# Two query tiles' attention weights turned in one PSUM bank, and the second group's sample scores asked for between the two turns

## The chip, the core and the metric

The kernel runs on one core of one Trainium2 chip. The core has five engines that run side by side, each through its own list of instructions in order: TensorE (PE in the profile; its weight loads are shown apart as PEld), VectorE (DVE), ScalarE (ACT), GpSimd (POOL) and SyncE (SP, which issues DMAs). They wait for one another through semaphores. The metric is the device time of one execution in microseconds (us).

## The reference, cut to what matters

One step of a two-layer encoder: a recurrent layer, then a layer of stick-breaking attention with 16 heads of 128, over 512 prompt rows and over 8 sample sequences of 16 rows, each with 512 cached rows. The change lies in the attention:

```python
def sb_block(q, q_pos, k, v):
    z = jnp.einsum('bqhd,bshd->bhqs', q, k).astype(jnp.float32) * (HEAD_DIM ** -0.5)
    mask = jnp.arange(k.shape[1])[None, :] < q_pos[:, None]
    log_keep = jnp.where(mask, jax.nn.log_sigmoid(-z), 0.0)
    log_after = lax.cumsum(log_keep, axis=3, reverse=True) - log_keep
    attn = jnp.where(mask, jnp.exp(jax.nn.log_sigmoid(z) + log_after), 0.0)
    o = jnp.einsum('bhqs,bshd->bqhd', attn, v.astype(jnp.float32))
    return o.astype(q.dtype)
# prompt: q, k, v of its own 512 rows; sample b: k, v of cache_k[b], cache_v[b] and 16 new rows
# y = (o * silu(zg)) @ w_out, where q and zg come from hn @ w_in
```

## The kernel before

The attention goes head by head. While one head's attention runs, TensorE also computes the next head's query and gate columns (`query`, a generator; its products are the matmuls `psh`, each 128x320, in fp32r with high and low parts, three matmuls for one product). `heads` walks a list of letters, `ORDER` for heads 0 to 14 and `LAST` for head 15, and calls one step for each letter:

- `q`: the next piece of the generator.
- `P` (`prompt_scores`): scores z3, z2, z1 of the four query tiles of 128 rows and, in z1, of the sample rows against their new keys; `sticks` then makes weights e of them (absolute value, exp, log on ScalarE, a scan and two subtractions on VectorE, exp on ScalarE, a mask on POOL). e3 holds query tile 3, e2 tile 2 and, in its last 128 columns, tile 0, and e1 tile 1.
- `S0`, `S1` (`sample_scores`): scores of 4 sample sequences against their cached keys (`zc`, tiles `ck`), and their weights by `sticks`.
- `V0`, `V1` (`prompt_turn`): the weights are turned (transposed through TensorE against `ident`) by `spread`: into a PSUM bank `pa`, split from there into a high part `ath` (ScalarE) and a low part `atl` (VectorE). V0 turns query tiles 3 and 2, V1 tiles 0 and 1.
- `O` (`prompt_out`): the prompt's output `po`, 12 matmuls over key blocks 0 to 3; block 0 reads row 0 of `ath` and `atl`, block 1 row 1, and so on.
- `T0`, `T1` (`sample_turn`): issues the loads of a group's cached values (`cv`, two tiles of 512 KB, two buffers, on SP's queue), turns the group's weights into banks `pas` (copied to `at` by ScalarE) and `pan` (copied to `an` by VectorE).
- `M0`, `M1` (`sample_out`): the group's output `pos`, first from `vn` and `an`, then 16 matmuls from `cv` and `at`. `C0`, `C1` (`sample_close`): turned back through `pot`, times the gate.
- `L`, `U`, `N`, `K`, `W`: loads and splits of the next head's keys and values (`kr`, `vr`, `ck`).

`pa`, `pas`, `pan`, `po`, `pos` and `pot` all come from one ring of two PSUM banks (`bank`, tag "one"). A bank is free again when its last reader is done. The letters are not the engines' order: a scheduler with costs and priorities of its own merges all steps into one list for each engine and picks, for each bank asked for, the one that it expects free. That is why the order is shown below from the built programs.

Of the kernel before, what the change touches and what calls it, by code (L numbers as in the profile page):

```python
# [11 lines left out]
F32 = mybir.dt.float32  # L12
F32R = mybir.dt.float32r
BF16 = mybir.dt.bfloat16
AF = mybir.ActivationFunctionType
ALU = mybir.AluOpType
# [3 lines left out]
P = 128  # L20
# [25 lines left out]
X12, X22, X11, S1, S2, S3, S4 = range(7)  # L46
# [4 lines left out]
class Trunk:  # L51
# [705 lines left out]
    S0 = 3 + TP  # L757
# [924 lines left out]
    def attention(self, h, ap, qkv, zs):  # L1682

        nc, I, O = self.nc, self.I, self.O
        V, A, mm, tr = nc.vector, nc.scalar, nc.tensor.matmul, nc.tensor.transpose
        kw = dict(skip_group_check=True)
        dma = nc.sync.dma_start
        one = self.bank
        zt = lambda n: self.ring("quad", 4, n)
        pd = "p (t d) -> p t d"  # L1690
# [9 lines left out]
        ath = ap.tile([P, 3, 512], F32R, tag="ath", name="ath", bufs=1)  # L1700
        atl = ap.tile([P, 3, 512], F32R, tag="atl", name="atl", bufs=1)

        def spread(e, i):

            ps = one("pa")
            for j in range(i + 1):
                tr(ps[:, P * j : P * j + P], e[:, P * j : P * j + P], self.ident)
            n = min(i + 1, 3)
            src = ps[:, : P * n].rearrange(pd, d=P)
            for sv, hv, lv in [(src, ath[:, :n, P * i : P * i + P], atl[:, :n, P * i : P * i + P])] + (  # L1710
                [(ps[:, 384:], ath[:, 1, 0:P], atl[:, 1, 0:P])] if i == 3 else []
            ):
                A.activation(hv, sv, AF.Copy)
                V.tensor_tensor(lv, sv, hv.bitcast(F32), ALU.subtract)


        def sample_scores(g):
# [10 lines left out]
        def new_values(g):  # L1728
            t = ap.tile([TS, 4, P], F32, tag="vn", name="vn", bufs=1)
            dma = (nc.gpsimd if g else nc.sync).dma_start  # L1730
            rows = O["v"][TP + 64 * g : TP + 64 * g + 64, P * h : P * h + P]
            dma(t, rows.rearrange("(b t) d -> t b d", t=TS))
            return t
# [72 lines left out]

        def prompt_turn(late):
            if late:
                spread(st["e2"][:, 384:], 0)
                spread(st["e1"], 1)  # L1810
            else:
                spread(st["e3"], 3)
                spread(st["e2"], 2)
# [12 lines left out]
        st = {"vn": new_values(0)}  # L1826
        steps = {"P": prompt_scores, "O": prompt_out}
        for g in range(2):
            steps[f"V{g}"] = lambda g=g: prompt_turn(g)
            steps[f"T{g}"] = lambda g=g: sample_turn(g)  # L1830
            steps[f"M{g}"] = lambda g=g: sample_out(g)
            steps[f"C{g}"] = lambda g=g: sample_close(g)
            steps[f"S{g}"] = lambda g=g: sample_scores(g)
# [2 lines left out]

    STAY = (NHEAD - 2,)
    LAST = "P S0 q q q S1 V0 q V1 q Z T0 M0 O q C0 q T1 q M1 q C1 q"
    ORDER = "P q q S0 L q q V0 V1 S1 T0 O U q M0 q T1 N K q C0 M1 W q C1"

    def heads(self, count=NHEAD):
        with self.pool("att") as ap:
# [10 lines left out]
            for h in range(count):  # L1853
# [3 lines left out]
                qn = self.query(h + 1, ap) if more else out  # L1857
                for step in (self.ORDER if more else self.LAST).split():
                    if step == "q":
# [152 lines left out]
```

## Time and profile before

| what | value |
|---|---|
| runs | 2860.42 us median of 3 (2860.24 to 2861.73) |
| profiled execution | 2859.51 us, its span 2857.4 us |
| PE busy | 2791.4 us, 98% of the span |
| VectorE, ScalarE, POOL busy | 71%, 58%, 15% |
| granted TensorE clock over the span | 0.995 |
| PE busy, 2230 to 2270 us (inside the heads) | 39.86 of 40.00 us |

The heads lie between about 2030 and 2640 us; one takes 39 us. PE works through them nearly without a gap, so the wait rows of PE and of its weight loads tell what is still open there. Line numbers (L1707) are those of the kernel before; L108 to L110 are the three matmuls of a product, L1707 the transposes of `spread`, L1713 and L1714 its splits, L1721 `zc`, L1745 and L1749 `pas` and `pan`, L1757 and L1762 `pos`, L1737 the loads of `cv`. In the changed kernel the lines behind `spread` are some nine higher.

### The profile page before, as it was taken

To read this page: it belongs to the slowest core of one execution; us is meant where nothing else is said; L and a number is where in the kernel's file an instruction comes from. 1 tells how busy PE (TensorE), PEld (TensorE's weight loads), DVE (VectorE), ACT (ScalarE), POOL (GpSimd) and SP (SyncE) were. 2 spreads that over 40 slices of the span, in tenths; PEclk is the share of its full clock that TensorE was granted. 3 is DMA by queue.
4 is the path that set the end of the run, shared out by engine and by line. 5 is a ranking of instruction groups with operands and counts; after the bars stand their busy time and mean duration, and the time that the engine had idled before them with its cause. 6 is when DMAs were issued, how large, how long until landed. Compare 5 with 4: busy or idle time off the path is not lost.

```text
span 2857.4 us, 48071 instructions
## 1 busy us (share of the span) xinstructions
PE 2791.4 (98%) x18340; PEld 2463.5 (86%) x18340; DVE 2033.8 (71%) x3344; ACT 1667.7 (58%) x2846; POOL 415.1 (15%) x684
## 2 busy tenths in 40 slices
PE   6899999999999999999999999999999999999998
PEld 5799999999999987777787899966889888887887
DVE  7677777777677766766866766667877877776335
ACT  5467556656566655665656555553666766666223
POOL 0021212122122211112220000001111111011000
PEclk9999999999999999999999999999999999999999
DMA  8966776667666666676786333574566666668637
GB/s 326 330 145 153 165 167 154 148 167 162 160 152 158 152 226 203 202 251 192 228 277 207 104 109 105 181 276 168 165 197 195 195 197 185 208 193 287 194 111 228
DMA packets 249094, 544.49 MB, mean 191 GB/s; under 512 B 23496, under 2 KB 108616, under 8 KB 247712
## 3 DMA queue, kind: packets, MB, share of 16 engines
q1 hardware_dynamic: 208528, 402.22, 43.6%
q0 software_dynamic: 40336, 139.21, 20.5%
q8 instruction: 144, 2.36, 0.3%
q14 instruction: 86, 0.70, 0.1%
HBM read 499.97 MB, written 41.37 MB: 189 GB/s over the span
## 4 chain that ended last, share of the span: by engine, by line
PE 80%; DVE 4%; ACT 4%; DMA 2%; issue 2%; POOL 0%; DVEq 0%; POOLq 0%; SPq 0%; ACTq 0%
PE acc L108 7%; PE acc L110 7%; PE acc L109 7%; PE pa L108 4%; PE pa L110 4%; PE pa L109 4%; PE psh L108 3%; PE psh L110 3%; PE psh L109 3%; PE pc L110 3%; PE pc L108 3%; PE pc L109 3%; PE acck L108 2%; PE acck L109 2%; PE acck L110 2%
## 5 line engine op out<-in xcount | busy, mean ns | idle before, releaser
L108 PE MATMUL acc<-wh,yh 128*128 128x512 f32 x940 | 370.3, 395 | 1.7 <-DVE e L1642 1.6
L109 PE MATMUL acc<-wl,yh 128*128 128x512 f32 x940 | 367.4, 391 | 0.4 <-DVE wl L94 0.4
L110 PE MATMUL acc<-wh,yl 128*128 128x512 f32 x940 | 366.2, 390 | 1.3 <-DVE yl L958 1.3
L94 DVE TENSOR_TENSOR wl<-wr,wh 128x1024 fp32r<-128x1024 f32 x151 | 186.6, 1238 | 217.6 <-ACT wh L93 216.9
L93 ACT ACTIVATE wh<-wr 128x1024 fp32r<-128x1024 f32 x151 | 159.5, 1057 | 264.7 <-PE acc L110 214.3
L108 PEld LDWEIGHTS acc<-wh,yh 128*128 128x128 f32 x940 | 176.6, 188 | 55.5 <-issue 16.1
L110 PEld LDWEIGHTS acc<-wh,yl 128*128 128x128 f32 x940 | 176.8, 188 | 38.6 <-DVE yl L958 1.7
L109 PEld LDWEIGHTS acc<-wl,yh 128*128 128x128 f32 x940 | 177.0, 188 | 37.5 <-DVE wl L94 1.1
L193 DVE TENSOR_TENSOR wa<-wa 128x1024 f32<-128x1024 f32 (+1 forms) x160 | 191.4, 1247 | 9.3 <-ACT wa L192 8.9
L110 PE MATMUL pa<-xs,wl 128*128 128x320 f32 x630 | 194.8, 309 | 0.5 <-DVE wl L94 0.5
L109 PE MATMUL pa<-xs,wh 128*128 128x320 f32 x630 | 194.7, 309 | 0.0
L108 PE MATMUL pa<-xs,wh 128*128 128x320 f32 x630 | 194.7, 309 | 0.0
L93 ACT ACTIVATE wh<-sum 128x896 fp32r<-128x896 f32 x102 | 96.8, 949 | 142.3 <-PE pa L109 46.5
L192 ACT ACTIVATE wa<-wa 128x1024 bf16<-128x1024 f32 x160 | 159.2, 1046 | 22.5 <-DVE wa L193 12.4
L542 POOL DMA_DIRECT2D sum<-w_in_a_dram x90 | 79.1, 882 | 498.2 <-DVE wl L94 237.7
L108 PE MATMUL psh<-nh,wl 128*128 128x320 f32 x480 | 150.8, 314 | 0.5 <-DVE z L1529 0.5
L110 PE MATMUL psh<-nh,wl 128*128 128x320 f32 x480 | 150.1, 313 | 0.0
L109 PE MATMUL psh<-nl,wl 128*128 128x320 f32 x480 | 149.4, 311 | 0.0
L93 ACT ACTIVATE wh<-rv 128x256 fp32r<-128x256 f32 (+1 forms) x108 | 51.8, 479 | 144.9 <-PE pa L109 92.3
L108 PE MATMUL acck<-wh,nh 128*128 128x512 f32 x320 | 127.5, 399 | 3.9 <-ACT nh L1163 2.2
L110 PE MATMUL pc<-xs,wl 128*128 128x320 f32 x420 | 129.8, 309 | 0.7 <-DVE wl L94 0.7
L108 PE MATMUL pc<-xs,wh 128*128 128x320 f32 x420 | 130.1, 310 | 0.0
(489 smaller groups left out, 8583.5 us busy)
## 6 DMA issues: line engine op xcount, KB each, us to landing
wa<-w_ada_dram SPq DMA_DIRECT2D x120, 512.0 KB, 6.1
wr<-w_out_a_dram SPq DMA_DIRECT2D x96, 512.0 KB, 4.5
sum<-w_in_a_dram POOLq DMA_DIRECT2D x90, 448.0 KB, 5.8
wa<-w_ada_dram POOLq DMA_DIRECT2D x72, 512.0 KB, 4.9
wr<-w_in_b_dram SPq DMA_DIRECT2D x64, 512.0 KB, 4.3
ck<-cache_k_dram SPq DMA_DIRECT2D x64, 512.0 KB, 5.0
cv<-cache_v_dram SPq DMA_DIRECT2D x64, 512.0 KB, 5.7
wr<-w_out_b_dram SPq DMA_DIRECT2D x55, 512.0 KB, 3.9
```

What stands on the lines that cost most here:

```text
L93: self.split_at = nc.scalar.activation(hi[:, :n], raw, AF.Copy).ins
L94: nc.vector.tensor_tensor(lo[:, :n], raw, hi[:, :n].bitcast(F32), ALU.subtract)
L108: mm(out, sh, mh, start=start, stop=False, **kw)
L109: mm(out, sh, ml, start=False, stop=False, **kw)
L110: return mm(out, sl, mh, start=False, stop=stop, **kw)
L192: nc.scalar.activation(parts[i], raw, AF.Copy)
L193: nc.vector.tensor_tensor(parts[2] if i else raw, raw, parts[i], ALU.subtract)
L542: self.nc.gpsimd.dma_start(self.big[tag], self.quarter(w, i), accum_op=ALU.add)
```

## The change

V1's two turns (tile 0 from e2, tile 1 from e1) put their three transposes into one bank instead of two. The splits from there are cut otherwise: first 256 columns, which are row 0 of `ath` and `atl` for tiles 0 and 1, then the 128 columns of row 1. And in `ORDER` the letter S1 goes ahead of V1 (`LAST` has that order already).

```diff
+        def parts(pairs):
+            for sv, hv, lv in pairs:
+                A.activation(hv, sv, AF.Copy)
+                V.tensor_tensor(lv, sv, hv.bitcast(F32), ALU.subtract)
+
         def spread(e, i):
             ps = one("pa")
             for j in range(i + 1):
                 tr(ps[:, P * j : P * j + P], e[:, P * j : P * j + P], self.ident)
-            n = min(i + 1, 3)
-            src = ps[:, : P * n].rearrange(pd, d=P)
-            for sv, hv, lv in [(src, ath[:, :n, P * i : P * i + P], atl[:, :n, P * i : P * i + P])] + (
-                [(ps[:, 384:], ath[:, 1, 0:P], atl[:, 1, 0:P])] if i == 3 else []
-            ):
-                A.activation(hv, sv, AF.Copy)
-                V.tensor_tensor(lv, sv, hv.bitcast(F32), ALU.subtract)
+            src = ps[:, :384].rearrange(pd, d=P)
+            parts([(src, *(x[:, :3, P * i : P * i + P] for x in (ath, atl)))]
+                  + [(ps[:, 384:], ath[:, 1, 0:P], atl[:, 1, 0:P])] * (i == 3))
+
+        def spread_first(e0, e1):
+            ps = one("pa")
+            for n, e in enumerate((e0, e1[:, :P], e1[:, P:])):
+                tr(ps[:, P * n : P * n + P], e, self.ident)
+            parts([(ps[:, : 2 * P], ath[:, 0, : 2 * P], atl[:, 0, : 2 * P]),
+                   (ps[:, 2 * P : 3 * P], ath[:, 1, P : 2 * P], atl[:, 1, P : 2 * P])])
...
             if late:
-                spread(st["e2"][:, 384:], 0)
-                spread(st["e1"], 1)
+                spread_first(st["e2"][:, 384:], st["e1"])
...
-    ORDER = "P q q S0 L q q V0 V1 S1 T0 O U q M0 q T1 N K q C0 M1 W q C1"
+    ORDER = "P q q S0 L q q V0 S1 V1 T0 O U q M0 q T1 N K q C0 M1 W q C1"
```

On TensorE, from V0's turns to the second group's `pas`, as in each of the heads 1 to 13; the query matmuls `psh` are left out where the dots stand. Before, there are 5, 5, 5, 4, 1, none and 16 of them in the seven gaps (the one behind the first `po` row holds only the other rows of `po`, and `pos` from `vn`):

```order
L1707 MATMUL pa<-ident,e 128x128 x7
L1721 MATMUL zc<-ck,qs 32x512 x4
...
L1707 MATMUL pa<-ident,e 128x128
...
L1707 MATMUL pa<-ident,e 128x128 x2
...
L1745 MATMUL pas<-ident,e 128x128 x4
...
L1749 MATMUL pan<-ident,e 16x128
...
L108 MATMUL po<-ath,vh 128x512
...
L1762 MATMUL pos<-cv,at 32x128 x16
...
L1745 MATMUL pas<-ident,e 128x128 x4
```

The same stretch of the changed kernel, with 5, 4, 5, 5, none, 10, none and 7 `psh` in the gaps:

```order
L1712 MATMUL pa<-ident,e 128x128 x7
L1730 MATMUL zc<-ck,qs 32x512 x4
...
L1721 MATMUL pa<-ident,e 128x128 x3
...
L1754 MATMUL pas<-ident,e 128x128 x4
...
L1758 MATMUL pan<-ident,e 16x128
...
L108 MATMUL po<-ath,vh 128x512
...
L108 MATMUL po<-ath,vh 128x384
...
L109 MATMUL po<-atl,vh 128x384
...
L1771 MATMUL pos<-cv,at 32x128 x16
...
L1754 MATMUL pas<-ident,e 128x128 x4
```

`zc` stays where it was, V1's transposes stand together, ten `psh` stand inside `po`, and of the 36 `psh` from `zc` to the second `pas` 29 are ahead of the first `pos` instead of 20.

On VectorE, from the 256-wide low split of V1 on, head 4 (`e<-zc` and `e<-z` are the second group's sample weights, `e<-keep` their scan, `wh` and `wr` the next head's query weights):

```order
L1714 TENSOR_TENSOR atl<-pa,ath 128x2x128
L1363 TENSOR_TENSOR wh<-wr,wh 128x512
L1636 SCALAR_TENSOR_TENSOR e<-z_22268,e 128x16
L1751 COPY an<-pan 16x128
L1639 SCALAR_TENSOR_TENSOR e<-keep_19843,e 128x528
L1374 TENSOR_TENSOR wr<-wr 128x512
L1642 TENSOR_TENSOR e<-zc,e 128x512
L1642 TENSOR_TENSOR e<-z_22268,e 128x16
L1820 TENSOR_TENSOR z<-po,z 128x512
```

```order
L1706 TENSOR_TENSOR atl<-pa,ath 128x256
L1636 SCALAR_TENSOR_TENSOR e<-zc,e 128x512
L1636 SCALAR_TENSOR_TENSOR e<-z_22264,e 128x16
L1760 COPY an<-pan 16x128
L1639 SCALAR_TENSOR_TENSOR e<-keep_19843,e 128x528
L1363 TENSOR_TENSOR wh<-wr,wh 128x512
L1642 TENSOR_TENSOR e<-zc,e 128x512
L1642 TENSOR_TENSOR e<-z_22264,e 128x16
L1706 TENSOR_TENSOR atl<-pa,ath 128x128
```

The last low split of V1 (row 1 of `atl`), which ended V1's work before the chain, now stands behind the whole chain.

On ScalarE, the same place:

```order
L1713 ACTIVATE ath<-pa 128x128
L1633 ACTIVATE e<-e 128x528
L1713 ACTIVATE ath<-pa 128x2x128
L1524 ACTIVATE z<-psh 128x320
L1362 ACTIVATE wh<-wr 128x512
L1747 ACTIVATE at<-pas 128x512
```

```order
L1705 ACTIVATE ath<-pa 128x256
L1633 ACTIVATE e<-e 128x528
L1756 ACTIVATE at<-pas 128x512
L1524 ACTIVATE z<-psh 128x320
L1362 ACTIVATE wh<-wr 128x512
L1705 ACTIVATE ath<-pa 128x128
```

The copy `at` has moved up by two, and the last high split of V1 stands behind it. In the built programs `pan` waits before for the 2x128 low split (its bank was V1's second) and now for `at` (its bank was that of `pas`).

## The prediction

> **What bounds the kernel now.** I read the page first, then the waits of the attention stretch, then one head's timeline engine by engine, then the DMA queue. The page's span, busy shares and chain:
>
> ```profile
> span 2857.4 us, 48071 instructions
> ...
> PE 2791.4 (98%) x18340; PEld 2463.5 (86%) x18340; DVE 2033.8 (71%) x3344; ACT 1667.7 (58%) x2846; POOL 415.1 (15%) x684
> ...
> PE 80%; DVE 4%; ACT 4%; DMA 2%; issue 2%; POOL 0%; DVEq 0%; POOLq 0%; SPq 0%; ACTq 0%
> ```
>
> TensorE (PE) is busy 98% of the span and carries 80% of the chain, so an edit is worth what it takes from or adds to PE's own stalls. Weight-load (PEld) waits in the attention stretch (2030 to 2640 us), and one of the SP queue (2050 to 2600); columns: total us, times, longest:
>
> ```profile
> PEld po L108 <- ACT at L1747: 2.6, 13, 0.2
> PEld pan L1749 <- issue: 4.0, 12, 0.4
> PEld pos L1762 <- DMA cv<-cache_v_dram: 0.9, 4, 0.3
> SPq L1737 <- PE pos L1762: 24.8, 28, 2.1
> ```
>
> Three stalls lie near the change: `po` and `pan` wait for a bank (6.6 us in all), and `pos` for cached values in only 4 of its 32 groups. SP's load of cached values (L1737) itself waits for the `pos` before it, because `cv` has two buffers. Heads 1 to 13 (counted from 0) issue in one order; I use head 5. PE:
>
> ```profile
> 2240.10 0.27 PE L1707 MATMUL pa<-ident,e 128*128 128x128 f32 x1
> ...
> 2241.04 0.44 PE L1707 MATMUL pa<-ident,e 128*128 128x128 f32 x2
> ...
> 2241.47 0.31 PE L110 MATMUL psh<-ks,wh 128*128 128x320 f32 x1
> ...
> 2241.91 0.31 PE L110 MATMUL psh<-nh,wl 128*128 128x320 f32 x1
> 2242.06 0.60 PE L1745 MATMUL pas<-ident,e 128*128 128x128 f32 x4
> ...
> 2242.93 0.31 PE L108 MATMUL psh<-nh,wl 128*128 128x320 f32 x1
> 2243.38 0.27 PE L1749 MATMUL pan<-ident,e 128*16 128x128 f32 x1
> 2243.41 0.39 PE L109 MATMUL psh<-nl,wl 128*128 128x320 f32 x1
> 2243.77 0.50 PE L108 MATMUL po<-ath,vh 128*128 128x512 f32 x1
> ...
> 2244.76 0.34 PE L109 MATMUL po<-atl,vh 128*128 128x384 f32 x1
> ...
> 2245.84 0.42 PE L1757 MATMUL pos<-vn,an 16*32 16x128 f32 x8
> 2246.19 1.08 PE L1762 MATMUL pos<-cv,at 128*32 128x128 f32 x32
> 2247.20 0.41 PE L110 MATMUL psh<-nh,wl 128*128 128x320 f32 x1
> ...
> 2249.66 0.60 PE L1745 MATMUL pas<-ident,e 128*128 128x128 f32 x4
> ...
> 2254.27 0.97 PE L1762 MATMUL pos<-cv,at 128*32 128x128 f32 x28
> ```
>
> A query matmul (`psh`) steps by 0.147 us (2241.47 to 2241.91, three steps). So `pan` stands 0.45 - 0.15 = 0.30 us late, and `po` 0.36 - 0.15 = 0.21.
>
> ScalarE (ACT) and VectorE (DVE) at the same place:
>
> ```profile
> 2241.32 0.26 ACT L1713 ACTIVATE ath<-pa 128x128 fp32r<-128x128 f32 x1
> 2241.47 0.64 ACT L1633 ACTIVATE e<-e 128x528 f32<-128x528 f32 x1
> 2242.01 0.38 ACT L1713 ACTIVATE ath<-pa 128x256 fp32r<-128x256 f32 x1
> ...
> 2243.11 0.61 ACT L1747 ACTIVATE at<-pas 128x512 f32<-128x512 f32 x1
> ```
>
> ```profile
> 2240.69 0.29 DVE L1714 TENSOR_TENSOR atl<-pa,ath 128x128 fp32r<-128x128 f32 x1
> ...
> 2242.82 0.41 DVE L1714 TENSOR_TENSOR atl<-pa,ath 128x256 fp32r<-128x256 f32 x1
> ...
> 2243.96 0.27 DVE L1751 COPY an<-pan 16x128 f32<-16x128 f32 x1
> 2244.16 1.23 DVE L1639 TENSOR_TENSOR_SCAN e<-keep,e 128x528 f32<-128x528 f32 x1
> 2245.32 0.66 DVE L1374 TENSOR_TENSOR wr<-wr 128x512 f32<-128x512 f32 x1
> 2245.90 0.67 DVE L1642 TENSOR_TENSOR e<-zc,e 128x512 f32<-128x512 f32 x1
> ```
>
> The `pan` wait ends with VectorE's 256-wide copy (2242.82 + 0.41 = 2243.23), the last reader of a `pa` bank; the `po` wait with ScalarE's `at` copy (2243.72), the last reader of the `pas` bank.
>
> The SP queue in head 5, then the `cv` tile's two loads there, then landing times min/median/max of the pairs issued in the middle of heads 1, 5, 7 and 8:
>
> ```profile
> 2245.94 0.37 SPq L1663 DMA_DIRECT2D vr<-out_v_dram  x1
> 2247.30 0.99 SPq L1737 DMA_DIRECT2D cv<-cache_v_dram  x2
> 2253.53 0.34 SPq L1350 DMA_DIRECT2D wr<-w_in_b_dram  x1
> ```
>
> ```profile
> L1737 SPq DMA_DIRECT2D cv<-cache_v_dram x2: 368/472/575, 2247.3 to 2247.7; - x2
> ```
>
> ```profile
> DMA to landing us min/median/max: 5.1/5.7/6.2
> DMA to landing us min/median/max: 4.5/5.1/5.7
> DMA to landing us min/median/max: 4.0/4.6/5.2
> DMA to landing us min/median/max: 4.1/5.5/6.8
> ```
>
> The second load of head 5 lands at 2247.7 + 5.7 = 2253.4; the second group's `pos` starts at 2254.27. That margin of 0.9 us decides my forecast.
>
> **The change part by part.** *Work.* The same ten transposes, five splits on ScalarE and five on VectorE per head, of the same widths in sum; one claim of the two-bank ring fewer. A transpose costs PE the same 0.11 us wherever it stands (2242.06 to 2242.93 holds four and three `psh` steps: 0.87 - 0.44 = 0.43). 0.
>
> *The score matmuls.* S1 ahead of V1 in the step list does not move `zc` on PE: it stands behind the seven `pa` in both orders. What moves is behind them. VectorE now runs the sample chain (scan, subtractions) ahead of the last split of the shared bank; ScalarE runs `at` two places earlier, and that bank's last 128 columns behind it; PE runs 9 more `psh` (29 for 20) ahead of the first group's `pos`, 10 of them inside `po`, and 9 fewer (7 for 16) behind it.
>
> *PE's bank waits, head 5, worked forward.* Three `pa` at 2240.10, four `psh`, and `pas` at 2241.12 (it takes the bank that VectorE's copy of 2240.69 frees at 2240.98). ScalarE: the 256-wide split at 2241.32; a step starts 0.11 before the end of the one ahead (2241.32 + 0.26 against 2241.47), so the 528-wide step at 2241.59 and `at` at 2242.12, to 2242.73. `pan` now takes the `pas` bank: 2242.88, with the same 0.15 from copy to PE as today, where five `psh` behind `pas` would let it start at 2242.30. Its wait grows from 0.30 to about 0.58. `po` starts at 2243.73 without a wait, its first four run for 0.99 us (2243.77 to 2244.76 today), then ten `psh` to 2246.19. VectorE: `an` at 2243.19, scan at 2243.39, 1.16 us to its successor (2244.16 to 2245.32), 0.60 each for a weight split and the subtraction (neighbours overlap by 0.08: 2245.32 + 0.66 against 2245.90) and under 0.1 for a 16-wide one, so the last split runs from 2245.8 to 2246.1. `po` goes on at 2246.22 and 1.08 us later (2244.76 to 2245.84 today) comes `pos`: 2247.3. With nine more `psh` (1.32) the old place would be 2247.16. So the bank waits end 0.15 us per head worse: 13 x 0.15 = 2.0 us. Bounds: if all of the two old waits went and no new one came, -6.6 us; if `pan` and the last split were each 0.2 later still, 13 x 0.55 = +7. I keep +2.0, since each step of it goes by rows of this head.
>
> The Trainium skill (Perfetto Trace Analysis, Matmuls under Optimizing Tensor Performance) advises that independent groups rotate through different PSUM banks so that evacuating one overlaps the next; by that the shared bank, held until its last split at 2246.10, leaves one bank for `pas`, `pan` and `po`, which speaks for the larger `pan` wait and against a gain of 6.6 us.
>
> *The cached values.* The first group's `pos` starts 1.47 us later, and SP issues the second group's `cv` loads only behind it. From its start to the issue: 2247.30 - 2246.19 = 1.11 us; 0.4 to the second issue; then the landing time x. From its start to the second group: 2254.27 - 2246.19 = 8.08, now less 1.32 = 6.76, and 0.10 more before the second tile is read. PE thus waits x + 1.51 - 6.86 = x - 5.35. The maxima of heads 1 to 13 are 6.2, 6.3, 5.7, 5.7, 5.7, 5.8, 5.2, 6.8, 5.6, 5.5, 6.1, 5.6, 5.7 (rows of four above): waits 0.85, 0.95, four of 0.35, 0.45, 0, 1.45, two of 0.25, 0.15, 0.75, together 6.5 us. Head 8's 0.3 is there already: +6.2. No `psh` can fill that in: PE runs its instructions in the program's order. Bounds: 0 if the later loads land 1.5 us sooner; +13 if each lands half a microsecond later. I take the rows' own landing times.
>
> *Other.* SP's order of loads does not change; the values load `vr` (L1663) also goes 1.4 us later, with its split needed only a head on. On POOL the second group's mask goes ahead of the `vn` load, and is ready by then. Heads 0, 14 and the last: 0, with 1 us either way.
>
> Sum: 2.0 + 6.2 = +8.2 us. The profiled execution took 2859.51 us (span 2857.4 and 2.1 around it): 2867.7. The median of the runs is 0.9 higher, so 2868.6 by it; I say 2868.3.
>
> **Rivals.** *Faster: the bank claim was the limit.* `pan` and `po` find free banks and the loads stay hidden: -6.6, 2853.8. For it: the two waits recur in 12 and 13 heads. Against: `pan` waits for `at` instead, and the margin of 0.9 is smaller than the shift of 1.32. It decides if the second load lands within 5.3 us of its issue; of 13 rows one does. Chance 0.08.
>
> *The same: the waits trade.* `pan` waits no longer than now and `po` loses its 0.21: 13 x 0.21 = -2.7 against +6.2, +3.5; or the loads, now clear of the cached-key loads, land 0.3 us sooner, 12 x 0.3 = 3.6 off, +4.6. 2861 to 2866. This also holds if only the merging took effect. Chance 0.28.
>
> *Worse: the shifted load meets the next one.* SP issues `wr` at 2253.53, and `cv` now ends near 2254.9: 1.4 us of overlap. Shared evenly that costs about 0.5 us per head: +6.5 more, 2875. Chance 0.1. The Trainium skill (DMA: Bandwidth & Descriptors, Queues, rings and completion order) has each DMA engine take one queue's descriptors in ring order, by which `wr` cannot go ahead and this term is 0, the sum staying at +8.2. The trace agrees as far as it goes: the pair of head 5 lands in order, 2251.8 and 2253.4.
>
> **How the numbers follow.** Mine 0.54, worse 0.10, same 0.28, faster 0.08. About 0.2% (5.7 us) is what a measurement of this kernel tells from no change: mine and the worse one are over it, 0.64. My own case spans 2866 to 2872; the range 2861 to 2875 takes in the second and third rival and leaves out the faster one.
>
> **What would show it.** Right: `pos` L1762 waits for `cv` in some 12 heads with 6 to 8 us in all; PE's wait before `pan` is released by `at`; `po` waits for the last `atl` split; heads 1 to 13 each some 0.6 us longer. Wrong: `cv` landing under 5.3 us after its second issue, or `pan` starting right behind its `psh`.

## The result, and the profile after

| | before | changed |
|---|---|---|
| median of the runs | 2860.33 us of 6 | 2871.96 us of 6 |
| ratio of the runs | | 1.0052, 95% interval 1.0038 to 1.0065 |
| profiled execution, span | 2859.51, 2857.4 us | 2871.99, 2869.8 us |
| PE's wait for cached values, 2030 to 2640 us | 0.9 us | 11.9 us |

The change made the kernel slower by 0.52%, or 14.9 us (11 to 19) by the ratio of the runs; the two medians lie 11.6 us apart. In a later comparison the changed kernel stood at 1.0041 (1.0028 to 1.0054). The forecast was +8.2 us. The page of the changed kernel: the span, the busy engines, and shares of the chain that ended last.

```profile
span 2869.8 us, 48053 instructions
...
PE 2792.9 (97%) x18340; PEld 2461.1 (86%) x18340; DVE 2035.0 (71%) x3344; ACT 1666.5 (58%) x2846; POOL 416.9 (15%) x684
...
PE 74%; ACT 5%; DVE 5%; DMA 5%; issue 3%; POOL 0%; SPq 0%; DVEq 0%; POOLq 0%; ACTq 0%
```

PE has 1.5 us more busy time in a span that is 12.4 us longer: the loss is waiting. On the chain DMA went from 2% to 5%, VectorE and ScalarE from 4% to 5% each. The weight-load waits of the attention stretch (2030 to 2640 us; total us, times, longest):

```profile
PEld pos L1771 <- DMA cv<-cache_v_dram: 11.9, 17, 1.5
PEld pan L1758 <- issue: 7.4, 14, 0.7
PEld po L109 <- DVE atl L1706: 2.4, 13, 0.2
PEld pas L1754 <- DVE atl L1706: 1.1, 4, 0.4
```

The three steps that the forecast named are here: `pos` waits for cached values in 17 places instead of 4, `pan` waits longer than its 4.0 us, and `po` now waits in its middle (L109) for the last `atl` split. The small wait of `pas` is new. Head 5 again, on PE (start us, length us), with the wait that the trace puts before an instruction in brackets:

```profile
2243.70 0.52 PE L1721 MATMUL pa<-ident,e 128*128 128x128 f32 x3
...
2244.64 0.60 PE L1754 MATMUL pas<-ident,e 128*128 128x128 f32 x4
...
2246.38 0.27 PE L1758 MATMUL pan<-ident,e 128*16 128x128 f32 x1 [0.40 <-ACT at L1756]
...
2247.21 0.40 PE L108 MATMUL po<-ath,vh 128*128 128x512 f32 x1
...
2249.64 0.44 PE L109 MATMUL po<-atl,vh 128*128 128x384 f32 x1
...
2250.82 0.42 PE L1766 MATMUL pos<-vn,an 16*32 16x128 f32 x8
2251.18 1.08 PE L1771 MATMUL pos<-cv,at 128*32 128x128 f32 x32
...
2257.97 0.41 PE L1771 MATMUL pos<-cv,at 128*32 128x128 f32 x4
2259.50 1.07 PE L1771 MATMUL pos<-cv,at 128*32 128x128 f32 x28 [1.11 <-DMA cv<-cache_v_dram]
```

VectorE's two low splits of V1, with the scan and the wide subtraction of the second group between them, and the SP queue in the same head:

```profile
2245.24 0.42 DVE L1706 TENSOR_TENSOR atl<-pa,ath 128x256 fp32r<-128x256 f32 x1
...
2246.89 1.24 DVE L1639 TENSOR_TENSOR_SCAN e<-keep,e 128x528 f32<-128x528 f32 x1
...
2248.64 0.67 DVE L1642 TENSOR_TENSOR e<-zc,e 128x512 f32<-128x512 f32 x1
...
2249.32 0.27 DVE L1706 TENSOR_TENSOR atl<-pa,ath 128x128 fp32r<-128x128 f32 x1
```

```profile
2250.93 0.37 SPq L1663 DMA_DIRECT2D vr<-out_v_dram  x1
2252.28 1.00 SPq L1746 DMA_DIRECT2D cv<-cache_v_dram  x2
2257.21 0.34 SPq L1350 DMA_DIRECT2D wr<-w_in_b_dram  x1
```

`cv` is again issued 1.1 us behind the start of the first group's `pos`, but the second group now starts 6.79 us after that start instead of 8.08, and finds its second tile missing: it runs four matmuls and waits until 2259.50.

Taken apart by the starts on PE, heads 1 to 13 (from the first `zc` of head 1 to that of head 14) took 508.1 us before and 525.8 now, 17.7 more; the expectations below have 507.4 and 525.0 for them. The stretch of the change (from the start of the last group of `zc` to the second `pas`, less the first group's `pos`) is, summed over these heads, 131.0 before and 134.8 now: +3.8, the banks. The second group's `pos` takes 1.16 us where it waits for nothing; beyond that it took 0.3 us before and 13.3 now, again in sum: +13.0, the cached values. The rest is +0.9. The profiled execution lost only 12.4 us in all, since its stretches ahead of head 1 and from head 14 on were some 5 us shorter than those of before. Two profiles of one kernel differ there as much: in the second one of the changed kernel the same stretches are 7 us longer than in the first.

### The profile page after: what moved, and what is told of

Its sections match the earlier page's. It is cut to its first block, busy times and chain, and to the rows that moved or that the text cites. A ratio compares the mean times of both kernels' runs of the same rounds, so it can differ in the third digit from the quotient of the medians.

```text
span 2869.8 us, 48053 instructions
## 1 busy us (share of the span) xinstructions
PE 2792.9 (97%) x18340; PEld 2461.1 (86%) x18340; DVE 2035.0 (71%) x3344; ACT 1666.5 (58%) x2846; POOL 416.9 (15%) x684
## 3 DMA queue, kind: packets, MB, share of 16 engines
q1 hardware_dynamic: 208528, 402.22, 43.5%
## 4 chain that ended last, share of the span: by engine, by line
PE 74%; ACT 5%; DVE 5%; DMA 5%; issue 3%; POOL 0%; SPq 0%; DVEq 0%; POOLq 0%; ACTq 0%
PE acc L108 7%; PE acc L110 7%; PE acc L109 7%; PE pa L108 4%; PE pa L110 4%; PE pa L109 4%; PE pc L110 3%; PE pc L108 3%; PE pc L109 3%; DMA cv<-cache_v_dram 2%; PE acck L108 2%; PE acck L109 2%; PE acck L110 2%; PE psa L230 2%; PE psh L108 2%
## 5 line engine op out<-in xcount | busy, mean ns | idle before, releaser
L109 PE MATMUL acc<-wl,yh 128*128 128x512 f32 x940 | 366.8, 390 | 0.3 <-DVE wl L94 0.2
L109 PEld LDWEIGHTS acc<-wl,yh 128*128 128x128 f32 x940 | 176.5, 188 | 37.5 <-DVE wl L94 1.5
L109 PE MATMUL pa<-xs,wh 128*128 128x320 f32 x630 | 194.7, 309 | 0.0
L109 PE MATMUL psh<-nl,wl 128*128 128x320 f32 x480 | 148.4, 309 | 0.0
```

The costliest lines, as they stand in the source:

```text
L109: mm(out, sh, ml, start=False, stop=False, **kw)
```

## The experiments

Theory A: the loss is the second group's cached values, asked for too late; the banks cost a little. Theory B: the loss is the banks, held by the late split. All times below are medians, with the ratio to the kernel before in the same comparison; "stretch" and "cv" are the two sums over heads 1 to 13 from above, from the profile of each kernel. `psh` are the query matmuls.

| kernel | time us | ratio (95%) | stretch | cv |
|---|---|---|---|---|
| before (first profile) | 2857 to 2860 | 1 | 131.0 | 0.3 |
| changed | 2871.96 | 1.0052 (1.0038 to 1.0065) | 134.8 | 13.3 |
| changed, again | 2869.89 | 1.0041 (1.0028 to 1.0054) | 134.1 | 11.5 |
| swap of S1 and V1 alone | 2858.97 | 1.0003 (0.9992 to 1.0014) | 130.8 | 1.5 |
| shared bank alone | 2865.12 | 1.0025 (1.0014 to 1.0037) | 137.4 | 1.6 |
| changed, no second load | 2865.81 | 1.0031 (1.0020 to 1.0043) | 133.2 | 0 |
| before, no second load | 2860.20 | 1.0013 (1.0002 to 1.0023) | 132.0 | 0 |
| changed, no second load but in the last head | 2862.03 | 1.0014 (1.0006 to 1.0023) | 134.9 | 0 |
| changed, early first group | 2863.30 | 1.0018 (1.0009 to 1.0026) | | |
| before, early first group | 2858.01 | 0.9999 (0.9990 to 1.0007) | | |
| changed, late second group | 2862.15 | 1.0015 (1.0004 to 1.0025) | 135.8 | 0.6 |
| changed, row 1 split first | 2855.46 | 0.9995 (0.9986 to 1.0004) | 130.8 | 1.7 |
| row 1 first and late second group | 2862.56 | 1.0013 (1.0004 to 1.0022) | 133.8 | 0 |
| before, swap and early first group | 2859.64 | 1.0003 (0.9994 to 1.0012) | | |

(With M0 ahead of O the stretch holds other work, and no sum is given.)

**The two halves apart.** The swap alone, on the kernel before:

```diff
-    ORDER = "P q q S0 L q q V0 V1 S1 T0 O U q M0 q T1 N K q C0 M1 W q C1"
+    ORDER = "P q q S0 L q q V0 S1 V1 T0 O U q M0 q T1 N K q C0 M1 W q C1"
```

> The kernel before with the new step order alone (S1 ahead of V1); V1 still turns into two banks. Theory A (late loads: the loss comes from PE's place of the first group's pos, which sets when the second group's cached values are asked for, and less from the banks): this step order leaves the first pos where it was on PE (20 psh behind zc), so no change, 2860 us within 3, and pos waits for cv in at most 5 groups. Theory B (banks: the last split of V1 behind the second group's sample chain holds a bank, and pan, po and pas pay): the last split already moves here, so 2862 to 2866.

No change: 1.0003. The expectation for theory B said that the last split moves here already; it does not, it stays ahead of the scan, so this run says only that the step order by itself is harmless.

The shared bank alone, on the changed kernel:

```diff
-    ORDER = "P q q S0 L q q V0 S1 V1 T0 O U q M0 q T1 N K q C0 M1 W q C1"
+    ORDER = "P q q S0 L q q V0 V1 S1 T0 O U q M0 q T1 N K q C0 M1 W q C1"
```

> The changed kernel with the old step order (V1 ahead of S1): one bank for V1's turns stays. On PE the first group's pos now stands behind 23 psh, where before has 20 and the changed kernel 29. Theory A: the wait per head is x - 6.2 by the prediction's sum (x the landing time of the second load; before x - 6.67, changed x - 5.35): 1 us in all by the landing times of before, 4 us by those of the changed kernel; with up to 3 us of bank waits 2861 to 2866, clearly under the changed kernel. Theory B: the shared bank is here in full, so most of the loss: 2867 to 2872.

The total came as theory A said, half the loss, but not its parts. The first `pos` starts 7.64 us ahead of the second, as the sum had it, and `cv` costs 1.6 us. The banks cost 6.4 us, against 3.8 and 3.1 in the two profiles of the changed kernel; 2.3 of them are what heads 5 and 8 alone take beyond the mean of the other eleven. Weight-load waits, 2030 to 2640 us:

```profile
PEld pan L1758 <- issue: 7.0, 15, 0.7
PEld po L109 <- DVE atl L1706: 5.0, 13, 0.4
PEld pas L1754 <- DVE atl L1706: 3.2, 5, 1.2
...
PEld pos L1771 <- DMA cv<-cache_v_dram: 1.2, 3, 0.6
```

Here only four `psh` stand inside `po` instead of ten, and the last split, now between the scan and the subtraction, is waited for 0.4 us in each of 13 heads instead of 0.2. Both theories are partly right so far.

**The loads taken away.** In both kernels:

```diff
-            st["cv"] = [cached_values(4 * g + 2 * u) for u in range(2)]
+            if g == 0:
+                st["cv"] = [cached_values(4 * g + 2 * u) for u in range(2)]
```

> The changed kernel without the loads of the second group's cached values: the second group multiplies with the first group's cached values (so its sample rows are computed from the wrong cache rows). Theory A: the 13 us that pos loses in heads 1 to 13 go, 2857 to 2861; against the kernel before without the same loads +2 to +5, which is what the banks cost. Theory B: the banks' price stays, 8 to 12 us over the kernel before without the same loads.

> The kernel before, likewise without the loads of the second group's cached values (second group computed from the first group's cache rows). Both theories: its pos waits for cv are only 0.9 us in all, so 2856 to 2860. Theory A says the changed kernel without the loads is 2 to 5 us above this one; theory B 8 to 12.

Heads 1 to 13 took 510.0 us and 508.7: of the 17.7 us between the two kernels 1.3 are left. The two times lie 5.6 us apart, just over theory A's 2 to 5 and under theory B's 8 to 12. By themselves they say less (theory A's 2857 to 2861 was missed by 5 us), since both kernels grew elsewhere: the last head follows another list, and behind its last `pos` the tail took 215.8 and 214.1 us where it takes 205.7 in the kernel before. So the changed kernel ran once more with the load kept in the last head (`if g == 0 or h == NHEAD - 1`):

> The changed kernel without the loads of the second group's cached values in heads 0 to 14, while the last head keeps its load (the second group of the other heads is computed from the first group's cache rows). Leaving it out in the last head too made the tail behind the attention some 8 us longer in both kernels, which hid what the heads gained. Theory A (late loads): heads 1 to 13 take 510 us as in the run without any second load (507.4 before, 525.0 changed), and with the tail as it was the time is within +1 to +5 us of the kernel before. Theory B (banks): +8 to +12 us.

1.0014, 4 us over before (1.7 to 6.6), inside theory A's 1 to 5. Its heads 1 to 13 took 511.9 us rather than the 510 expected, its tail is back at 205.9, with the stretch at 134.9, as in the changed kernel with its loads:

```profile
PEld pan L1759 <- issue: 7.9, 14, 0.7
...
PEld po L109 <- DVE atl L1706: 2.4, 13, 0.2
PEld pas L1755 <- DVE atl L1706: 1.7, 6, 0.7
```

The bank waits stand and `cv` is gone, and with it 0.27 to 0.38 points of the 0.41 to 0.52%.

**The wait moved instead.** The first group earlier, on the changed kernel and on the kernel before (there with V0 V1 S1):

```diff
-    ORDER = "P q q S0 L q q V0 S1 V1 T0 O U q M0 q T1 N K q C0 M1 W q C1"
+    ORDER = "P q q S0 L q q V0 S1 V1 T0 M0 O q q T1 U N K q C0 M1 W q C1"
```

> The changed kernel with the first group's output M0 ahead of the prompt's output O in the step list, and the values load U behind T1, so that the load of the second group's cached values isn't queued behind it. All loads stay. On PE the first pos comes ahead of po, 3.5 us further from the second pos: by the sum the wait is x - 8.9, under every landing time seen. Theory A: pos for cv waits 0, heads 1 to 13 take 508 to 512 us, the time 2857 to 2863 (before 2857 to 2860 in these comparisons). Theory B: the shared bank and its late split are as in the changed kernel, so 2866 to 2872.

> The kernel before with the same two moves as the changed kernel with the early group (M0 ahead of O, U behind T1). It shows what these moves cost or bring by themselves: theory A takes the pos waits of before (0.9 us in all) and up to 0.4 us of head 8 away and leaves the banks, 2856 to 2861, within 3 us of before. Beside it the changed kernel with the early group shows the price of the shared bank alone: theory A 1 to 4 us, theory B 8 to 12.

All loads stay, and the loss falls to 0.18%, 0.3 us over the expected 2857 to 2863. Only one load is waited for, 1.0 us, ahead of 2066 us, in head 0:

```profile
PEld pan L1758 <- issue: 7.7, 15, 0.7
PEld pa L1721 <- issue: 4.3, 6, 1.7
...
PEld pas L1754 <- DVE atl L1706: 1.9, 5, 0.7
PEld pos L1771 <- DMA cv<-cache_v_dram: 1.0, 1, 1.0
```

The move alone costs the kernel before nothing (0.9999), so the shared bank with its late split is worth 2863.3 - 2858.0 = 5.3 us, a little over the 1 to 4 that theory A gave. The second group later, on the changed kernel:

```diff
-... q C0 M1 W q C1"
+... q C0 W q M1 C1"
```

> The changed kernel with the second group's output M1 one step later in the list, 12 psh (1.76 us) further from the first: the wait is x - 7.1, so almost none. Theory A: pos for cv 0 to 1 us in all; the turn back pot, now two matmuls behind pos, waits up to 0.3 us per head for ScalarE's ob copy, 4 us in all; 2859 to 2866. Theory B: as the changed kernel, 2866 to 2874.

2862.15, in theory A's range: three different ways of taking the wait for `cv` away (no load, an earlier release, a later use) end within 1.3 us of each other, at +0.14 to +0.18%.

**The split's place.** What is left, some 4 to 5 us, should be theory B's. On the changed kernel the two splits of the shared bank change places:

```diff
-            parts([(ps[:, : 2 * P], ath[:, 0, : 2 * P], atl[:, 0, : 2 * P]),
-                   (ps[:, 2 * P : 3 * P], ath[:, 1, P : 2 * P], atl[:, 1, P : 2 * P])])
+            parts([(ps[:, 2 * P : 3 * P], ath[:, 1, P : 2 * P], atl[:, 1, P : 2 * P]),
+                   (ps[:, : 2 * P], ath[:, 0, : 2 * P], atl[:, 0, : 2 * P])])
```

> The changed kernel with the two splits of the shared bank in the other order, the 128 columns of row 1 ahead of the 256 of row 0. On PE po then starts later and the first pos stands behind 23 psh instead of 29, 7.64 us from the second: the wait per head is x - 6.1. Theory A: 1.5 to 4 us of cv waits and 2 to 7 us for the banks, 2861 to 2868, between before and the changed kernel. Theory B (the late split behind the sample chain is what costs): with that split now ahead of the scan the loss is gone, 2857 to 2861.

The whole loss is gone: 0.9995, under theory A's range and just under theory B's. The first `pos` stands 7.64 us ahead of the second, as expected, and `cv` costs 1.7 us. But the banks cost nothing: the stretch is 130.8, and the rows of `pan` and `po` are those of the kernel before (4.0 in 12, 2.6 in 13) to 0.2 us:

```profile
PEld pan L1758 <- issue: 3.9, 12, 0.4
PEld po L108 <- ACT at L1756: 2.8, 13, 0.2
...
PEld pos L1771 <- DMA cv<-cache_v_dram: 1.8, 4, 0.7
```

In head 5 of this kernel both low splits are done before the scan:

```profile
2239.55 0.29 DVE L1706 TENSOR_TENSOR atl<-pa,ath 128x128 fp32r<-128x128 f32 x1
2240.85 0.41 DVE L1706 TENSOR_TENSOR atl<-pa,ath 128x256 fp32r<-128x256 f32 x1
2241.18 1.25 DVE L1639 TENSOR_TENSOR_SCAN e<-keep,e 128x528 f32<-128x528 f32 x1
```

and the built program has no `psh` inside `po`. From the changed kernel this one differs by the order of the two splits alone, and nearly all of both losses goes with it. "Shared bank alone" has the same bank, the same three transposes and the same 7.64 us, and takes 6.6 us more in the stretch (it also has the old step order, which cost nothing by itself). So the shared bank itself is free, and the row 1 split behind the second group's scan is what is paid for, once in the banks and once more through the `psh` that stand ahead of the first `pos`. That the scheduler put them into `po` because it saw the split coming late fits the three programs (ten with the split behind the subtractions, four with it behind the scan, none ahead of it), but its reasons were not looked into.

**Repeated, and joined.** The changed kernel a second time:

> The changed kernel once more, beside the next two, with a second profile of it. Theory A in its present form: the second group's loads land 5.3 to 6.0 us after their issue, and 6.5 us or later where a 16 KB packet of the instruction queue falls into the load; heads 2, 5, 8 and 11 again lose most, pos waits 11 to 14 us in heads 1 to 13 in all (cv rows beyond 1.16 us per head), the ratio to before is 1.004 to 1.0065. Rival: those four heads were chance of one execution, and others are long this time.

11.5 us for `cv`, and again heads 2, 5, 8 and 11 are the longest: 41.7, 43.5, 41.0 and 40.2 us, the other nine 39.4 to 40.0. Both repeat, so they were not the chance of one execution of this kernel.

Two more kernels joined what had cost nothing, in search of one that beats both:

> The kernel before with S1 ahead of V1, M0 ahead of O and U behind T1; two banks for V1's turns. It joins the two edits that cost nothing: the swap alone had 2.9 us less wait before po and pan, the early group no cv wait. If both add up 2854 to 2857, 0.1% under before; if the banks' waits come back at another place, as before within 2 us.

> The changed kernel with both costs taken away at once: the row 1 split first (the run before lost nothing to the banks and 1.5 us to cached values in five heads) and the second group's output M1 a step later (12 psh further from the first, so the wait is x - 7.9, under every landing time but the longest). Theory A with the split order in it: no cv wait, heads 1 to 13 in 506 to 508 us (507.4 before), 2854 to 2858, no difference from before that can be told, at best 0.1% under it. If the shared bank has a price of its own that the split order only moved, over 2860.

Neither does. The first is as before (1.0003): the second load now has 0.6 to 1.8 us to spare, but `pos` waits for ScalarE instead (7.5 us in 13 heads in the same rows). The second missed its expectation of 2854 to 2858 by 5 us, though no head waits for `cv` beyond the first:

```profile
PEld pa L1721 <- issue: 5.9, 13, 0.9
PEld pot L1778 <- ACT ob L1774: 3.8, 15, 0.5
```

```profile
PE pa L1721 <- DVE atl L1706: 2.9, 13, 0.7
```

V1's three transposes now wait in 13 places, for a low split of VectorE by PE's own row (the second fence); with row 1 first alone their weight loads wait 1.4 us in two places, and in the changed kernel with the late group 5.3 in 12. So the late second group has a price of its own at V1, which my expectation left out: in head 5 V0's wide low splits start 1.87 us behind V0's first transpose there, and 1.47 with row 1 first alone. Why VectorE comes later was not looked into. No kernel tried beats the one before by more than can be told.

## Why the prediction was right or wrong

**The mechanism was right; the step that failed is the size of the cached-values term.** The loss is PE's wait for the second group's cached values and a smaller one for banks. The forward working of head 5 holds: counted from its `pa`, `pas` was put at +1.02 us, `pan` at +2.78, `po` at +3.63, its second half at +6.12 and the last split at +5.7; the trace has +0.94, +2.68, +3.51, +5.94 and +5.62. The order of the queue, the 1.11 us from `pos` to the issue and the distances between the groups (6.76 us forecast here, 7.64 by the same sum for the shared bank alone) came out within 0.03 us. The heads grew by 1.4 us in the mean, not by the 0.6 forecast.

**The banks, 2.0 us forecast, 3.8 and 3.1 measured.** The changed side came out: my working put the first `pos` (from `vn`) 7.20 us behind V1's `pa`, which in head 5 of before starts 1.83 behind the start of the last group of `zc`, 9.03 in all; the mean over 13 heads of the changed kernel is 9.04. That it agrees to 0.01 is luck: the mean is made of 1.92 and 7.12, and single heads take 8.63 to 9.37. Wrong was the other side of the difference: I took head 5 as the old time, 7.57 us, and the mean of the 13 heads is 7.43. In heads like 3 and 4 `pan` hardly waits, so head 5 was 0.14 us above the mean: 13 x 0.14 = 1.8 us. Heads differ there by up to 0.5 us, so a difference of 0.15 can't be taken from one of them.

**The cached values, 6.2 us forecast, 13.0 and 11.2 measured.** This is the step that failed, and that made the size wrong: the wait and its place are right, its two inputs are not. By the formula x - 5.35 with the landing times of the changed kernel's own profile the waits are 10.7 us where I had 6.5, so 4.2 come from x, and 2.6 from the constant, 0.2 us a head: the 0.10 that I gave for reaching the second tile was not there to be had, 0.05 goes from landing to the next matmul (2259.45 to 2259.50 in head 5), and the last 0.05 I can't place. I took the landing times of one execution of before as they stood; the loads of heads 2, 5, 8 and 11 land later in the changed kernel (7.1, 6.8, 8.0 and 6.7 us against 6.3, 5.7, 6.8 and 6.1) and bring 8.5 of the 13.3 us. That they do so because they are asked for later is not shown: with the swap alone, where the groups stand 8.08 us apart as before, heads 2, 5 and 8 took 7.0, 6.8 and 7.4 us, and the formula with that profile's landing times gives 8.5 us instead of 6.5. So a part of the miss lies, as far as these runs show, in having read one execution in which the loads landed early. The upper bound of this term, +13 if each load lands half a microsecond later, was where it ended, but not by its condition: the loads landed 0.3 us later in the mean (6.17 against 5.85 us), and the constant gave the rest.

**The rivals.** "Faster" failed where its price said: `pan` waited for `at`, and of the 13 loads none landed within 5.3 us. "The same" failed with it. "Worse: the shifted load meets the next one" gave 2875, near the result, but not for its reason. The overlap was there: in head 5 `wr` is issued at 2257.21 and the tiles land at 2257.9 and 2259.5. But in head 2 the first 4 KB packet of `wr` starts at 2135.7, and the last rows of `cv` go on to 2136.8 at the pace they had before it, one in 0.025 us. The trace agrees with the ring order that the Trainium skill states (DMA: Bandwidth & Descriptors, Queues, rings and completion order), as far as a trace can that doesn't name the engine of a packet.

The rotation of banks that the Trainium skill advises (Perfetto Trace Analysis, Matmuls under Optimizing Tensor Performance) is not what was paid for: with row 1 split first one bank serves both turns at no cost (0.9995).

**What no step of mine held:** that the order of two splits within the new function decides all of it. I took the place of the last split as part of the change, and priced its bank and its 0.03 us of wait in `po`, not the ten query matmuls that moved ahead of it.

## What to carry to other kernels

Two loads that share their buffers with the group before are asked for when that group's last reader is done, so whatever moves that reader later or the next user earlier eats the margin; before such a move, compare the margin with the whole spread of the landing times, not with one. When an order is made by a scheduler, the order of two small splits on one engine can rearrange another engine's program (here ten query matmuls inside `po`, or none), so it is worth trying both. A difference of tenths of a microsecond per turn needs the mean over the turns on both sides.

## What the hardware showed that was not expected

A single 16 KB packet on the instruction queue goes along with a late 512 KB load. The DMA rows of head 2 (late) and head 3 in the changed kernel, each 7.7 us from the issue of `cv` on: mean busy share of the 16 DMA engines in 40 slices, GB/s, and for head 2 the instruction packet, which head 3 doesn't have.

```profile
DMA  7799645145789999999999998752100977897897
GB/s 221 207 332 295 194 101 98 56 88 141 215 250 279 330 356 346 341 348 346 418 282 277 279 295 237 186 133 64 21 11 21 213 234 234 255 295 253 362 386 277
...
q8 instruction: 1, 0.02, 0.9%
```

```profile
DMA  9995736947999999999999997521008937595987
```

```profile
DMA to landing us min/median/max: 6.0/6.6/7.1
```

```profile
DMA to landing us min/median/max: 4.1/4.8/5.4
```

In head 2 the packet starts 3.7 us after the issue and takes 1.16 us, while rows of 512 B take about 0.03. Two thirds along the GB/s row the rate falls to 21 and 11 GB/s, about a sixteenth of the 340 ahead of it. That fits one engine that goes on alone with its rows while the other 15 have none left of `cv`; the trace doesn't name the engine of a packet. The second load lands after 7.1 us, and after 5.4 in head 3 (the two landing rows, head 2 ahead of head 3), where the zeros are the time between the end of `cv` and the next load. Over heads 1 to 13 of the eleven profiles that have these loads (ten kernels, the changed one twice), 53 second loads had such a packet between 0.5 us before and 4.5 us after the pair's issue, and landed a median of 6.4 us after their own issue; 29 of them took over 6.3. The other 90 landed at 5.6, and 5 took over 6.3. With the window 0.4 us later the medians change by 0.1. The trace doesn't say whose instructions the packet carries, and no run moved it, so this is a coincidence seen often rather than a cause that was tested. The Trainium skill (DMA: Bandwidth & Descriptors, Queues, rings and completion order) has a DMA engine drain a whole packet of one queue before it turns to the next; the 1.16 us that this packet took agree with that, though no run shows which engine took it.
